# S5 maps: lag products and DRAM copies moved into the third MLP; norm squares first; results stored by token of the chunk

## Chip, cores and metric

One core of a Trainium2 chip runs the whole kernel as one program. The metric is the device time of one execution in microseconds. A profile of one execution goes with it; its times are us from the start of the profiled span.

## What is computed

A trunk of four layers over 256 tokens with 1024 channels. Each layer is a mixer and an MLP, each between two norms (`h += norm(mixer(norm(h)))`, the same for the MLP). The mixers are gated spatial mixing, pooling, latent attention and an S5 state-space layer; the change concerns what is prepared for the last one. Cut to that:

```
def rmsnorm(x, g):
    return x * rsqrt(mean(x * x, axis=-1) + 1e-6) * g

for i in range(4):
    z = mixer[i](rmsnorm(h, norm_g[i, 0]))
    h = h + rmsnorm(z, norm_g[i, 1])
    z = rmsnorm(h, norm_g[i, 2])
    z = square(relu(z @ w_up[i])) @ w_down[i]        # 1024 -> 4096 -> 1024
    h = h + rmsnorm(z, norm_g[i, 3])

def s5_mixer(h, ...):       # 64 groups of 16 channels, a complex state of 64 each
    dt = exp(log_dt); ab = exp(lam * dt); f = (ab - 1) / lam
    bu = (f * b) @ u                                  # per group
    x[t] = ab * x[t - 1] + bu[t]                      # scan over the tokens
    y = real(c @ x) + d_skip * u
    y = gelu(y)
    return (y @ w_glu_a) * sigmoid(y @ w_glu_b)
```

## The kernel before

The sublayers run one after another: `Gmlp`, `Mlp` 0, `Pooling`, `Mlp` 1, `Attention`, `Mlp` 2, `S5`, `Mlp` 3 (text below: first to fourth MLP). Tokens are in two blocks of 128. Every large product is made of three fp32r products (high and low parts), so each weight tile is loaded through SP's queue into one of three raw buffers and split by ACT (high part, L341) and DVE (low part, L342) into one of eight weight places. An MLP has eight groups of 512 hidden channels: `up_units` (L296 through `mm3`, into `mm`) and `down_units` (into `acc`), 22 us a group.

`boundary` (L1765) runs a sublayer's body, and then its last products for block 1, beside which block 0 is already normed, added and lifted (transposed) for the next sublayer; block 1 follows within the next body, after a first product of block 0 (`head`).

S5 doesn't scan token by token. It works in chunks of eight tokens and needs three sets of maps that depend on its parameters alone: `d_f` (into the state), `d_m` (within a chunk) and `d_e` (out of the state), 4 MB each in DRAM. `Tables` makes them as background work, a generator that `Core.tick` steps between the matmul units by an estimated clock: `yield 14` asks for a pause of 14 us by that clock. Its work is emitted in the middle of the MLPs' work; then a scheduler that runs a timing model fixes the order of each engine's instructions at build time. An emission under `high_priority(offset=-LATER)` counts as 500 instructions later than it stands.

`Tables.maps` (L1660) loops over 16 chunks of groups. For each, POOL loads `bo`, `bt`, `pb`, computes `e` and `cb` (complex products, `cmul`, L1553 to L1558) and `f`, and stores `f` to `d_f` and part of `e` to `d_out` (L1690). After every second chunk, `lags` (L1712) multiplies `e` with `cb` of two chunks on PE, eight small fp32 products a step (16 records in the trace, 128x128 with 32 weight columns), into the one buffer `pf`; ACT copies it to `lags`, and `place` (L1724) arranges it on POOL and stores it to `d_lag`. At the end eight copies within DRAM make `d_m` from `d_lag` (L1706) and four make `d_e` from `d_out` (L1709). `emit` drains the background before the third MLP, so all of it is emitted by then. `S5.stream` loads maps from `d_m` and `d_e` straight into the eight weight places, ahead of use.

S5 needs `h` with tokens in chunk order. `reorder` (L449), emitted in the third MLP, stores `h` to `d_h` on POOL's queue and loads it back through `in_chunks`, whose first dimension is the four tokens s, the second 32 chunks j. `finish` (L459) stores the result through the same view, per block two halves of 512 columns, one on SP's queue and one on ACT's.

The norm behind a sublayer is `add_normed` (L394): `t` = z * g on DVE (L404), `sumsq` of z on ACT (L355) inside `rstd`, a short chain for the root (L366 to L384), `h` += t * q (L408). z is in PSUM except for S5.

## Time and profile before

| | us |
|---|---|
| median of 3 runs | 1115.44 (1115.24 to 1116.12) |
| the profiled execution | 1114.36 |
| its span | 1112.6 |
| PE busy | 1013.0 (91%) |
| DVE busy | 749.7 (67%) |
| ACT busy | 546.6 (49%) |
| POOL busy | 391.5 (35%) |
| DMA | 233.97 MB, 210 GB/s on the mean |

PE is the engine of the matrix products; most of the time it is the one that the others feed. Its idle time is therefore read first, by who released it; then the stretches in which it ran with a lowered clock; then the stages in which no product runs.

### The profile page before, as it was taken

The numbers are of one execution on the slowest core, as the hardware profiler recorded it, in microseconds if no ns is written. First come the engines' busy times: TensorE is split into PE (matmuls) and PEld (weight loads), VectorE is DVE, ScalarE is ACT, GpSimd is POOL, SyncE is SP. The second block draws the span as 40 slices with busy tenths as digits, with TensorE's granted clock in tenths as the row PEclk, the third lists the DMA queues.
The fourth block names the chain that finished last, engine by engine and source line by source line (L and its number), as shares of the span: only waits on it lengthen the run. The fifth ranks groups of instructions, "written<-read, shape, count | busy, mean of one in ns | idle before, by whom it ended". The sixth has DMA issues, their size and how long they took to land.

```text
span 1112.6 us, 16304 instructions
## 1 busy us (share of the span) xinstructions
PE 1013.0 (91%) x6345; PEld 888.9 (80%) x6345; DVE 749.7 (67%) x1127; ACT 546.6 (49%) x818; POOL 391.5 (35%) x592
## 2 busy tenths in 40 slices
PE   7898999999689998988799799999985998999994
PEld 5886998997579887877687688999863777899983
DVE  5879999755986773657875665656569577454552
ACT  6946464443464443434454455545423466354531
POOL 4000002612879999899889430000003000000000
PEclk9999999999789998999999989999998999999998
DMA  9665475667576665665763798764576444646431
GB/s 333 233 232 189 152 256 197 204 243 268 182 252 234 217 219 183 231 211 174 247 207 120 242 391 232 246 220 157 218 307 248 151 153 157 220 157 221 156 112 38
DMA packets 82606, 233.97 MB, mean 210 GB/s; under 512 B 6320, under 2 KB 9648, under 8 KB 80736
## 3 DMA queue, kind: packets, MB, share of 16 engines
q1 hardware_dynamic: 67256, 182.73, 47.7%
q0 software_dynamic: 14720, 49.60, 13.4%
q8 instruction: 50, 0.82, 0.3%
q10 hardware_dynamic: 552, 0.59, 0.1%
q14 instruction: 28, 0.23, 0.1%
HBM read 218.48 MB, written 27.00 MB: 221 GB/s over the span
## 4 chain that ended last, share of the span: by engine, by line
PE 57%; POOL 15%; DVE 12%; DMA 7%; ACT 4%; issue 3%; SPq 0%; DVEq 0%; POOLq 0%; ACTq 0%
PE acc L296 29%; PE mm L296 26%; DVE w L342 3%; DMA raw<-in_a_w_in 2%; POOL tmp L1557 2%; DMA d_f<-f 2%; DVE s L1273 2%; DMA raw<-in_w_down 1%; ACT w L341 1%; DMA raw<-in_w_up 1%; POOL tmp L1554 1%; PE pf L296 1%; DVE h L408 1%; ACT junk L355 1%; DVE w L340 1%
## 5 line engine op out<-in xcount | busy, mean ns | idle before, releaser
L342 DVE TENSOR_TENSOR w<-raw,w 128x1024 fp32r<-128x1024 f32 (+3 forms) x304 | 379.0, 1277 | 163.9 <-ACT w L341 162.8
L341 ACT ACTIVATE w<-raw 128x1024 fp32r<-128x1024 f32 (+3 forms) x304 | 309.0, 1044 | 239.6 <-PE acc L296 131.9
L296 PE MATMUL acc<-w,h1hi 128*128 128x512 f32 (+1 forms) x1312 | 403.0, 391 | 3.7 <-ACT h1hi L341 3.1
L296 PE MATMUL mm<-zhi,w 128*128 128x256 f32 x1920 | 357.1, 286 | 3.4 <-DVE s L823 2.4
L296 PEld LDWEIGHTS mm<-zhi,w 128*128 128x128 f32 x1920 | 304.9, 194 | 6.8 <-DVE s L823 2.6
L296 PEld LDWEIGHTS acc<-w,h1hi 128*128 128x128 f32 x1312 | 244.8, 190 | 54.2 <-ACT h1hi L341 4.8
L296 PE MATMUL mm<-zlo,w 128*128 128x256 f32 x960 | 273.4, 285 | 0.0
L296 PE MATMUL acc<-w,h1lo 128*128 128x512 f32 (+1 forms) x656 | 253.6, 391 | 1.5 <-DVE h1lo L342 1.5
L296 PEld LDWEIGHTS mm<-zlo,w 128*128 128x128 f32 x960 | 185.9, 194 | 1.5 <-issue 0.4
L296 PEld LDWEIGHTS acc<-w,h1lo 128*128 128x128 f32 x656 | 124.4, 190 | 28.7 <-DVE h1lo L342 2.4
L631 DVE TENSOR_TENSOR s<-s 128x512 f32<-128x512 f32 x56 | 43.3, 773 | 61.1 <-ACT s L630 61.1
L630 ACT ACTIVATE s<-mm 128x512 f32<-128x512 f32 x56 | 33.4, 596 | 73.3 <-PE mm L296 71.1
L342 DVE TENSOR_TENSOR h1lo<-s,h1hi 128x512 fp32r<-128x512 f32 x60 | 54.1, 904 | 21.4 <-ACT h1hi L341 21.4
L341 ACT ACTIVATE h1hi<-s 128x512 fp32r<-128x512 f32 x60 | 45.3, 757 | 27.4 <-DVE s L631 25.5
L1275 POOL MEMSET t<- 128x32 f32 x2 | 0.3, 168 | 151.6 <-DVE h L408 151.6
L296 PE MATMUL mm<-w,zhi 128*128 128x512 f32 x128 | 42.1, 411 | 2.6 <-DVE zlo L342 2.1
L355 ACT ACTIVATE junk<-acc 128x512 bf16<-128x512 f32 x28 | 16.7, 595 | 56.0 <-DVE t L404 55.9
L404 DVE TENSOR_TENSOR t<-acc,bc 128x512 f32<-128x512 f32 x28 | 19.0, 686 | 36.1 <-PE acc L296 36.1
L296 PE MATMUL acc<-w,zhi 128*128 128x512 f32 (+2 forms) x128 | 38.4, 382 | 1.6 <-ACT w L339 1.6
L431 PE MATMUL mm<-ident,t 128*128 128x128 f32 x86 | 14.2, 303 | 24.3 <-DVE t L421 19.7
L328 POOL DMA_DIRECT2D bc<-in_norm_g x15 | 8.4, 558 | 78.8 <-DVE t L404 30.5
L431 PEld LDWEIGHTS mm<-ident,t 128*128 128x128 f32 x86 | 11.2, 157 | 27.5 <-issue 25.8
(304 smaller groups left out, 1227.4 us busy)
## 6 DMA issues: line engine op xcount, KB each, us to landing
raw<-in_w_up SPq DMA_DIRECT2D x64, 1024.0 KB, 5.2
raw<-in_w_down SPq DMA_DIRECT2D x64, 1024.0 KB, 5.1
bc<-in_norm_g POOLq DMA_DIRECT2D x15, 512.0 KB, 4.7
raw<-in_a_w_in SPq DMA_DIRECT2D x7, 1024.0 KB, 8.9
bt<-in_k_bt POOLq DMA_DIRECT2D x16, 256.0 KB, 4.5
raw<-in_a_w_out SPq DMA_DIRECT2D x4, 1024.0 KB, 6.2
d_out<-e POOLq DMA_DIRECT2D x16, 256.0 KB, 2.8
d_pb<-d_pw POOLq DMA_DIRECT2D x8, 512.0 KB, 8.8
```

The source lines that it names most:

```text
L296: return self.nc.tensor.matmul(out, lhsT, rhs, start=start, stop=stop)
L340: return i, nc.vector.scalar_tensor_tensor(lo, src, gain, hi.bitcast(F32), op0=ALU.mult, op1=ALU.subtract)
L341: i = nc.scalar.activation(hi, src, AF.Copy)
L342: return i, nc.vector.tensor_tensor(out=lo, in0=src, in1=hi.bitcast(F32), op=ALU.subtract)
L355: self.nc.scalar.activation(self.junk[:, 0:x.shape[-1]], x, AF.Square, scale=scale, bias=shift, accum_out=ss[:, i:i + 1])
L404: nc.vector.tensor_tensor(tn, zn, gn, op=ALU.mult)
L408: nc.vector.scalar_tensor_tensor(hn, tn, q, hn, op0=ALU.mult, op1=ALU.add)
L431: self.nc.tensor.transpose(ps[:, k * 128:(k + 1) * 128], z[:, k * 128:(k + 1) * 128], self.ident)
L630: nc.scalar.activation(s, state[f], AF.Relu)
L631: nc.vector.tensor_tensor(s, s, s, op=ALU.mult)
L1273: tt = lambda o, x, y, op: nc.vector.tensor_tensor(o, x, y, op=op)
L1557: eng.tensor_tensor(t, xr, yi, op=ALU.mult)
```

## The change

Six things. (1) `maps` no longer multiplies lags: `e` and `cb` lie in one tile `ec` (704 columns), which is stored whole to `d_ec`. (2) A new generator `within` waits for `late`, set when the third MLP begins; it then fetches two chunks of `ec` at a time (one step ahead), multiplies the lags, places them, and after every second step makes a quarter of `d_e` by two copies within DRAM; there is a pause of 6 us after each part. At its end the eight copies make `d_m`. (3) The background is drained not before the third MLP but after that MLP's sixth up-projection (g == 6). (4) `reorder` loads `h` back in four pieces of 32 partitions a block. (5) `finish` stores each half block in four such pieces. (6) `add_normed` emits the squares before the products with the gain.

```diff
--- before.py
+++ after.py
@@ -27,6 +27,7 @@
 LN_2 = Fraction("0.69314718055994530941723212145817656807550013436")
 MAGIC = 1.5 * 2.0 ** 23
 TURN_MAX = 0.5 - 2.0 ** -24
+EC = 704
 FMAX = float(np.finfo(np.float32).max)
 
 N_W = 8
@@ -38,6 +39,7 @@
 DEPTH = 2
 N_MAPS = 3
 MAPS_US = 14
+LAGS_US = 6
 LATER = 500
 WARM_S5 = 7.5
 
@@ -212,7 +214,7 @@
         self.background = None
         self.ends = {}
         self.recent = []
-        self.shallow = False
+        self.shallow = self.late = False
         self.weights = Weights(self)
         nc = self.nc
         self.eps = self.const.tile([128, 1], F32, name="eps")
@@ -355,10 +357,10 @@
             self.nc.scalar.activation(self.junk[:, 0:x.shape[-1]], x, AF.Square, scale=scale, bias=shift, accum_out=ss[:, i:i + 1])
         return [ss[:, i:i + 1] for i in range(len(parts))]
 
-    def rstd(self, parts, inner=None, outer=None):
+    def rstd(self, sums, inner=None, outer=None):
 
         nc = self.nc
-        a, b = self.sumsq(parts, D ** -0.5)
+        a, b = sums
         v = self.tiny("v")
         if inner is None:
             nc.vector.tensor_scalar(v, a, b, EPS, op0=ALU.add, op1=ALU.add)
@@ -399,17 +401,18 @@
             inner, outer = self.tiny("r4"), self.tiny("r2")
             nc.vector.tensor_tensor(outer, r, r, op=ALU.mult)
             nc.vector.tensor_tensor(inner, outer, outer, op=ALU.mult)
+        ss = self.sumsq(z, D ** -0.5)
         t = self.tp.tile([128, D], F32, name="t")
         for tn, zn, gn in zip(halves(t), z, halves(g)):
             nc.vector.tensor_tensor(tn, zn, gn, op=ALU.mult)
         with self.chain():
-            q = self.rstd(z, inner, outer)
+            q = self.rstd(ss, inner, outer)
             for hn, tn in zip(halves(self.h[b]), halves(t)):
                 nc.vector.scalar_tensor_tensor(hn, tn, q, hn, op0=ALU.mult, op1=ALU.add)
 
     def factor(self, b):
 
-        return self.rstd(halves(self.h[b]))
+        return self.rstd(self.sumsq(halves(self.h[b]), D ** -0.5))
 
     def scaled(self, b, g, r=None, out=None):
 
@@ -453,14 +456,18 @@
         for b in range(NB):
             nc.gpsimd.dma_start(out=d[b * 128:(b + 1) * 128], in_=self.h[b])
         for b in range(NB):
-            nc.gpsimd.dma_start(out=self.h[b], in_=in_chunks(d)[b])
+            for s in range(4):
+                nc.gpsimd.dma_start(out=self.h[b][sl32(s)], in_=in_chunks(d)[b][s])
         self.chunked = True
 
     def finish(self, out):
+
+        nc = self.nc
         for b in range(NB):
-            o = in_chunks(out)[b] if self.chunked else out[b * 128:(b + 1) * 128]
-            for n, queue in enumerate((self.nc.sync, self.nc.scalar)):
-                queue.dma_start(out=o[..., 512 * n:512 * n + 512], in_=self.h[b][:, 512 * n:512 * n + 512])
+            for n, queues in enumerate(((nc.sync,) * 4, (nc.scalar,) * 4)):
+                c = slice(512 * n, 512 * n + 512)
+                for s, queue in enumerate(queues):
+                    queue.dma_start(out=in_chunks(out)[b][s][:, c], in_=self.h[b][sl32(s), c])
 
     def z_parts(self):
         hi = self.xp.tile([128, 8, 256], F32R, name="zhi")
@@ -677,6 +684,8 @@
         for g in range(1, NG):
             k.run(self.up_units(g), side)
             side = [(5.0, self.factors)] if g == 1 else ()
+            if self.i == 2 and g == 6:
+                k.drain()
             if g == 1 and self.next is not None:
                 self.next.start()
             w = self.take()
@@ -1439,7 +1448,7 @@
         self.d_pw = k.dram.tile([2, 8, 16, 256], F32, name="d_pw")
         self.d_pb = k.dram.tile([128, 2, 16, 256], F32, name="d_pb")
         self.d_lag = k.dram.tile([8, 128, 512], F32, name="d_lag")
-        self.d_out = k.dram.tile([128, 32, 2, 128], F32, name="d_out")
+        self.d_ec = k.dram.tile([128, 16, EC], F32, name="d_ec")
 
     def small(self, name, *shape):
         return self.k.pre_p.tile([128, *shape], F32, name=name)
@@ -1663,9 +1672,6 @@
         k, nc, a = self.k, self.nc, self.a
         fr, fi = self.f
         pr, pi = self.powers
-        lg = self.small("lg", 512)
-        nc.gpsimd.memset(lg, 0.0)
-        before, made = None, None
         for ch in range(16):
             qs = slice(2 * ch, 2 * ch + 2)
             bo = self.small("bo", 192)
@@ -1677,8 +1683,9 @@
             tmp = self.small("tmp", 256)
             fb = lambda t: t[:, qs, None].to_broadcast([128, 2, 16])
             self.cmul((ov[:, 0], ov[:, 1]), (bv[:, 0], bv[:, 1]), (fb(fr), fb(fi)), tmp[:, 0:32].rearrange("p (q c) -> p q c", q=2))
-            e, cb = k.mp.tile([128, 2, 2, 9, 16], F32, name="e"), k.mp.tile([128, 2, 2, 2, 16], F32, name="cb")
-            nc.gpsimd.memset(cb, 0.0)
+            ec = k.mp.tile([128, EC], F32, name="ec")
+            e, cb = self.parts_of(ec)
+            nc.gpsimd.memset(ec[:, 576:EC], 0.0)
             for g in range(2):
                 hs = slice(64 * g, 64 * g + 64)
                 nc.gpsimd.tensor_copy(cb[hs, :, :, g], ov[hs])
@@ -1687,27 +1694,50 @@
             self.cmul([e[:, :, r, 1:9] for r in range(2)], (wide(2), wide(3)), (pw(pr), pw(pi)), tmp.rearrange("p (q i c) -> p q i c", q=2, c=16))
             nc.gpsimd.tensor_copy(e[:, :, :, 0], bv[:, 2:4].rearrange("p n q c -> p q n c"))
             nc.gpsimd.tensor_scalar(e[:, :, 1], e[:, :, 1], -1.0, None, op0=ALU.mult)
-            nc.gpsimd.dma_start(out=self.d_out[:, qs], in_=e[:, :, :, 1:9].rearrange("p q r i c -> p q r (i c)"))
-            if made is not None:
-                self.place(lg, *made)
-                made = None
+            nc.gpsimd.dma_start(out=self.d_ec[:, ch], in_=ec)
             f = self.small("f", 4, 2, 64)
             self.cmul([f[:, :, r] for r in range(2)], (pb[:, 0], pb[:, 1]), (bt[:, 0], bt[:, 1]), tmp.rearrange("p (s m) -> p s m", s=4))
             nc.gpsimd.dma_start(out=k.d_f[:, 4 * ch:4 * ch + 4], in_=f.rearrange("p s r m -> p s (r m)"))
             yield MAPS_US
-            if ch % 2:
-                with k.tc.high_priority(offset=-LATER):
-                    made = ch // 2, self.lags((before, (cb, e)))
-            before = cb, e
             yield 0
-        self.place(lg, *made)
+
+    def parts_of(self, ec):
+
+        return ec[:, 0:576].rearrange("p (q r i c) -> p q r i c", q=2, r=2, c=16), ec[:, 576:EC].rearrange("p (r q g c) -> p r q g c", r=2, q=2, g=2)
+
+    def within(self):
+
+        k, nc = self.k, self.nc
+        lg = self.small("lg", 512)
+        nc.gpsimd.memset(lg, 0.0)
+        fetched = {}
+
+        def fetch(n):
+            fetched[n] = []
+            for ch in (2 * n, 2 * n + 1):
+                ec = k.mp.tile([128, EC], F32, name="ec")
+                nc.gpsimd.dma_start(out=ec, in_=self.d_ec[:, ch])
+                fetched[n].append(self.parts_of(ec)[::-1])
+
+        fetch(0)
+        yield LAGS_US
+        for n in range(8):
+            with k.tc.high_priority(offset=-LATER):
+                t = self.lags(fetched[n])
+            if n < 7:
+                fetch(n + 1)
+            yield LAGS_US
+            self.place(lg, n, t)
+            if n % 2:
+                r, g = n // 4, n // 2 % 2
+                src = self.d_ec[64 * g:64 * g + 64, :, 0:576].rearrange("p h (q r x) -> p h q r x", q=2, r=2)
+                for q in range(2):
+                    nc.gpsimd.dma_start(out=k.d_e[64 * r:64 * r + 64, 2 * q + g:64:4], in_=src[:, :, q, r, 16:144])
+            yield LAGS_US
         for i, s in enumerate(TOKEN):
             w = self.d_lag.rearrange("n (g c) f -> c (n g) f", c=16)[:, :, 256 * (s // 4) + 32 * (3 - s % 4):][:, :, 0:128]
             nc.gpsimd.dma_start(out=k.d_m[16 * i:16 * i + 16], in_=w)
-        for r in range(2):
-            for g in range(2):
-                nc.gpsimd.dma_start(out=k.d_e[64 * r:64 * r + 64, g:64:2], in_=self.d_out[64 * g:64 * g + 64, :, r])
-        yield 0
+            yield 3
 
     def lags(self, pairs):
 
@@ -1740,6 +1770,9 @@
         yield from self.recurrence()
         self.k.early = False
         yield from self.maps()
+        while not self.k.late:
+            yield 0
+        yield from self.within()
 
 
 def constants():
@@ -1797,7 +1830,7 @@
             while k.early:
                 k.step()
         if isinstance(s, Mlp) and s.i == 2:
-            k.drain()
+            k.late = True
         boundary(k, s, n)
     k.finish(out)
 
```

## Rows read from the trace of the kernel before

**Rows 1.** Page, part 2: busy tenths of the span in 40 slices of 27.8 us.
```profile
PE   7898999999689998988799799999985998999994
POOL 4000002612879999899889430000003000000000
```

**Rows 2.** Waits of PE: engine, line, releaser: us in total, times, longest.
```profile
PE pf L296 <- POOL e L1555: 15.4, 7, 5.4
...
PE pf L296 <- POOL e L1689: 3.2, 1, 3.2
```

**Rows 3.** Timeline of PE, 380 to 525 us: start, duration, instruction [idle before].
```profile
382.75 0.43 PE L296 MATMUL pf<-e,cb 128*32 128x128 f32 x8 [0.77 <-POOL e L1555]
...
429.31 0.66 PE L296 MATMUL pf<-e,cb 128*32 128x128 f32 x8 [5.43 <-POOL e L1555]
...
478.02 0.66 PE L296 MATMUL pf<-e,cb 128*32 128x128 f32 x8 [2.99 <-POOL e L1555]
...
502.33 0.41 PE L296 MATMUL pf<-e,cb 128*32 128x128 f32 x4 [0.52 <-POOL e L1555]
...
521.13 0.43 PE L296 MATMUL pf<-e,cb 128*32 128x128 f32 x8 [2.96 <-POOL e L1555]
```

**Rows 4.** Stretches, second and fourth MLP: busy us (instructions) by engine, clock, DMA, GB/s.
```profile
320.00:518.20 198.20, 188.45 (x1168) 165.80 (x1168) 124.54 (x124) 87.54 (x115) 185.14 (x277) 0.96 0.63 211
922.07:1098.60 176.53, 175.69 (x1096) 158.79 (x1096) 93.89 (x113) 79.06 (x100) 0.00 (x0) 1.00 0.46 157
```

**Rows 5.** The second MLP's stretch, tile pf alone: PE, weight loads, ACT.
```profile
320.00:518.20 198.20, 5.86 (x64) 2.00 (x64) 1.09 (x4) 0.96 0.63 211
```

**Rows 6.** Stretches behind two waits: columns as in rows 4.
```profile
430.00:435.00 5.00, 5.00 (x30) 4.99 (x30) 0.00 (x0) 0.00 (x0) 4.21 (x7) 0.68 0.43 157
520.00:525.00 5.00, 3.87 (x21) 3.68 (x22) 4.66 (x11) 1.45 (x5) 4.81 (x7) 0.70 0.81 265
```

**Rows 7.** Timelines of ACT and PE at the start of the third and fourth MLP.
```profile
637.16 1.06 ACT L341 ACTIVATE w<-raw 128x1024 fp32r<-128x1024 f32 x1 [6.89 <-DMA raw<-in_w_up]
...
642.26 1.94 PE L431 MATMUL mm<-ident,t 128*128 128x128 f32 x8 [8.22 <-DVE t L421]
...
922.07 1.23 PE L431 MATMUL mm<-ident,t 128*128 128x128 f32 x8 [2.10 <-DVE t L421]
```

**Rows 8.** Stretches at the start of the third MLP: columns as in rows 4.
```profile
640.00:645.00 5.00, 2.74 (x13) 2.66 (x14) 4.64 (x8) 1.60 (x3) 2.52 (x4) 0.50 1.03 420
645.00:650.00 5.00, 5.00 (x17) 3.95 (x17) 2.44 (x3) 2.22 (x3) 3.91 (x6) 0.67 1.02 406
```

**Rows 9.** DMA issues, whole run, then 600 to 700 us: KB each, us to landing.
```profile
raw<-in_w_up SPq DMA_DIRECT2D x64, 1024.0 KB, 5.2
...
d_e<-d_out POOLq DMA_DIRECT2D x4, 1024.0 KB, 10.4
d_m<-d_lag POOLq DMA_DIRECT2D x8, 512.0 KB, 14.2
```

**Rows 10.** The end: one stretch (as in rows 4); ACT's stores, ns min/median/max.
```profile
1107.00:1108.00 1.00, 0.00 (x0) 0.00 (x0) 0.00 (x0) 0.00 (x0) 0.00 (x0) 0.50 0.27 104
...
L463 ACTq DMA_DIRECT2D out<-h x2: 552/850/1147, 1093.1 to 1103.3; - x2
```

**Rows 11.** Page, part 5: the norm's squares; busy, mean ns, idle before, releaser.
```profile
L355 ACT ACTIVATE junk<-acc 128x512 bf16<-128x512 f32 x28 | 16.7, 595 | 56.0 <-DVE t L404 55.9
```

**Rows 12.** Low priority, and S5's first products: DVE timeline, tile pf, PE timeline.
```profile
200.91 0.83 DVE L1644 TENSOR_TENSOR t<-t 128x256 f32<-128x256 f32 x2
...
L1651 PE MATMUL pf<-ident,t x4: 270/270/272, 238.8 to 239.9; 128*128 128x128 f32 x4
...
829.30 1.12 PE L296 MATMUL mm<-raw,zlo 128*32 128x128 f32 x32 [1.35 <-issue]
...
835.04 1.47 PE L1343 MATMUL acc<-w,zlo 128*32 128x128 f32 x42
...
861.14 1.72 PE L296 MATMUL pf<-w,t 128*32 128x128 f32 x25 [8.71 <-DVE t L1273]
```

## What the change should do, by the rows

> **What bounds the kernel now.** I began with the busy slices of the page [rows 1]. TensorE (PE) is full in most slices, so what can be gained lies in its idle time and in stretches where it runs slowly; GpSimd (POOL) is nearly full from slice 11 to slice 21 and does nothing in most of the third MLP. Next the waits of PE, grouped by releaser [rows 2]: PE stood 15.4 + 3.2 = 18.6 us before the small "pf" matmuls until POOL had written `e`. These are the `lags` products, which the schedule placed into PE's order before POOL was done. The timeline of PE [rows 3] gives the places: 0.77, 5.43, 2.99 and 0.52 us in the second MLP, 2.96 us at its end, where attention begins; the other 5.9 us lie in pooling and attention. Then two MLPs with the same matrix work, from the transposes of their second block to the last product [rows 4]: 198.20 us for the second MLP, 176.53 us for the fourth. The 21.7 us between them is what the S5 preparation costs there. Two more places stand out: the 8.22 us before the third MLP's transposes [rows 7], and the end, where results are stored at 104 GB/s with the DMA engines 27% busy [rows 10].
>
> **Second MLP: -18 us.** The change takes the products out. (a) The four waits go: 0.77 + 5.43 + 2.99 + 0.52 = 9.7 us. (b) The products go: 64 records with 5.86 us of busy time in this stretch [rows 5]; they run one after another, so I take 5.5. (c) After the two long idles PE was granted 0.68 of full speed in 430 to 435 us [rows 6], a mean of its levels of 1.2 and 2.4 GHz, where the fourth MLP had 1.00 throughout [rows 4]: 0.32 x 5 = 1.6 us, and about as much after the 2.99 us wait, scaled by its length to 1.0; 2.7 us together. Sum 17.9. The bound above is the whole 21.7 us. Below, DVE's splitting of weights could come next: it is busy for 124.54 of 198.20 us [rows 4], and would be 69% busy in 180 us. PE recorded no long wait for a split here, so DVE keeps up on the mean; I bound the loss at half, 9 us. What else changes in the maps (one whole store of `ec` for the store of its part, no `place`, no wait for `lags`) only shortens POOL's list, whose end nobody on the path waits for.
>
> **Attention and pooling: -6 us.** At the start of attention 2.96 us goes, and with it the slow clock behind it (0.70 in 520 to 525 us [rows 6], 0.30 x 3.9 busy us = 1.2). What remains of the 18.6 us is 5.9, of which most stands in front of work that waits for DVE anyway; I count 2. The bounds are 2 (DVE's chain through the latents is late next) and 12 (all of the waits, their clock and the products' own time).
>
> **The boundary to the third MLP: -9.5 us.** PE waits 8.22 us for `t` of the second block. On ACT the square root of that chain sits behind a weight split, and the split waited 6.89 us for its weights [rows 7]. The DMA engines are full (share 1.03, in 640 to 645 us still [rows 8]): the four copies of `d_e` inside DRAM, 1 MB each and 10.4 us to land, have just been issued, and the w_up load shares with them; over the whole run such a load lands in 5.2 us [rows 9]. The change takes these copies away from here, spreads them by halves over the third MLP, and leaves only the two chunks of the first fetch. What is late next is the chain itself, acc to squares to root to `h` to transposes: the same boundary of the fourth MLP waits 2.10 us [rows 7]. So 8.2 - 2.1 = 6.1 us, plus the clock: 0.67 in 645 to 650 us, and 0.50, the lower level, over the 2.74 busy us before [rows 8], 0.33 x 5 + 0.50 x 2.74 = 3.0; after the 2.10 us wait it was not lowered. Sum 9.1, and 0.4 for DMA relief behind it. Bounds: 3 (the load is late for its slot, not for traffic) and 11.
>
> **Third MLP: +9 us.** All 128 records move here, where PE is full, so they cost in full: 2 x 5.86 = 11.7 us above, or, since with both chunks at hand the sixteen of one step run in a row (8 in 0.43 us [rows 3]), 16 x 0.43 = 6.9 below. I take 8. The new wait is for fetched data: sixteen loads of 352 KB on POOL's queue. I price a landing at the 5.2 us of a 1 MB weight load [rows 9]. The first steps are fetched one step (three pauses of 6 us) ahead, so nothing waits; the steps that the drain emits in a lump have no such lead, and the second buffer of each fetch is freed only by the products before (three buffers). I put 1 us there, 0 to 15.6 (three steps at 5.2). Behind a waiting DMA on POOL stand the bias and gain broadcasts and `place`; POOL is idle here [rows 1], and PE needs none of them in the MLP. The traffic is another 6 MB read, in a stage where the engines had room after the burst of its first 20 us. The reload of `h` in chunk order, now eight DMAs, is needed some 20 us later and hidden by the MLP's products; uncovered it would cost its landing, 5 us and up.
>
> **S5: +2 us.** Before, the maps were complete long ahead; S5's first product ran at 829.30 us and the first one with a map at 835.04 [rows 12]. Now the last three steps and the eight `d_m` copies are emitted with the sixth up-projection, two of eight groups before the MLP's end (2 x 176.5 / 8 = 44 us), and the products at low priority. What such a priority costs is shown once: the transposes of `spread` were ready at 201.7 (end of DVE's L1644) and ran at 238.8 [rows 12], 37 us later. So the last steps run as the MLP ends; then `place`, one store, eight copies, whose landing I take as 5 us rather than the 14.2 of the crowded stretch [rows 9]: `d_m` is there about 16 us after S5's first product instead of long before. PE's next hard wait, until 861.14 for DVE's scan [rows 12], ends 32 us behind that product and hides nearly all of it. I take 2, bounds -1 and 12.
>
> **The end: -3.3 us.** 27% of sixteen engines is four: each store has an outermost dimension of four (the token of the chunk). Cut into pieces of 32 partitions, the 512 KB can go over all: 6 us of transfer at 104 GB/s become 1.5 us at four times the rate. Against that stand three more issues on each queue, 0.55 us at the least [rows 10], 1.7 us, partly beside the transfer. Net 3.3; bounds 0 and 5. The Trainium skill agrees on the four ("DMA: Bandwidth & Descriptors", "Why a DMA increments its semaphore by 16 and not by 1": the slowest dimension sets how many engines a DMA gets). But its section "Rules for kernel authors" there speaks against cutting: transfers of disjoint partitions serialize, one of 128 partitions is better. By the first rule the end is shorter by my 3.3 us, by the second it stays as it is; the share of 27% bears out the first.
>
> **Squares before products in the norm: -0.5 us.** ACT's squares waited for DVE's `t` on the same bank, 55.9 us over the kernel [rows 11], nearly all off the path. Now `t` waits for the squares; on the path it is the same two operations in the other order, the root's first step a little earlier at best. Bounds -2 and +2.
>
> **Sum.** -18 - 6 - 9.5 + 9 + 2 - 3.3 - 0.5 = -26.3. The profiled execution took 1114.4 us, its span 1112.6 and 1.8 around it; 1114.4 - 26.3 = 1088. The median of the runs is 1.1 higher, so 1089.
>
> **Rivals.**
> (A) PE's wait moves with the products: instead of POOL it waits for the fetched chunks. For it: PE takes its instructions in order, and three steps come in a lump. Against: the first five are fetched early. Price 15.6 us instead of the 1 counted, and 3 of slow clock: 1107. Chance 0.13.
> (B) The maps come too late for S5; this ends slower. The chain from the last product to the last load of a map is serial: fetch, product, `place`, store, eight copies, eight loads of 1 MB. At the landings of the crowded stretch (14.2 for a `d_m` copy [rows 9], as much again for the store, 10 for each of two fetches) the last map lies about 80 us behind the MLP's end. It decides from about 40 us on, where DVE's scan no longer covers it; every us beyond is PE's, the weights behind it on SP's queue and the eight weight places held by maps too. To lose all of 26 us it must come 66 us late; at 80 us, 1089 + 40 - 2 = 1127. Against: the DMA engines are half empty then. Chance 0.08.
> (C) The second MLP is bound by splits, DVE being slowed by POOL's work that stays: half of the 18 us, 1098. Chance 0.13.
> (D) The boundary keeps its stall, the load being late for its slot: 1089 + 6 = 1095. Chance 0.08.
> (E) The end does not shorten, since pieces serialize: 1089 + 3.3 = 1092; small beside the rest. Chance 0.10. The second rule of the skill named above would do this.
>
> **How the numbers follow.** My forecast, 1089 give or take 10, has 0.48. A, C, D, E lie between 1092 and 1107 and are faster than before too. The range is 1076 (the good bounds of MLP, attention and end together) to 1107 (A included); B and sums better than 1076 are left out. A difference of 0.2%, 2.2 us, is about what a measurement of this kernel can tell from none. Faster 0.88, same 0.03 (B half way, or A with C), slower 0.09 (B and a bad order of instructions).
>
> **What would show it.** In the profile after: no PE wait for POOL's `e`; the second MLP near 180 us by the stretch of rows 4; the wait before the third MLP's transposes near 2 us and granted clock 1.00 behind it; "pf" products of `ec` in the third MLP with about 8 us, and no idle before them; the third MLP longer by these; S5's first use of a map at most 10 us later against its first product; the store at the end with a DMA share well above 0.27. It is wrong if PE waits for `ec`, for maps in S5, or if the second MLP stays above 189 us.

## The result, and the profile after

The changed kernel takes 1131.07 us (median of 4, 1126.15 to 1133.07) beside 1115.34 for the kernel before: a ratio of 1.0154, 95% interval 1.0118 to 1.0189. It is 16 us slower where I had forecast 26 us faster. The profiled execution took 1130.65 us, its span is 1128.7.

The stages, from the timelines of PE (us; a stage runs to the start of the next one; the columns e2 to e9 are experiments, told below):

| stage, from | before | after | e2 | e3 | e6 | e9 |
|---|---|---|---|---|---|---|
| start of the span | 320.0 | 319.7 | 320.3 | 318.2 | 320.5 | 319.1 |
| second MLP: transposes of its second block | 201.5 | 181.4 | 181.1 | 180.6 | 181.0 | 181.0 |
| attention: first 384-column product | 120.8 | 132.0 | 130.9 | 126.5 | 115.2 | 115.5 |
| third MLP: transposes of its second block | 187.0 | 206.9 | 190.8 | 186.3 | 205.8 | 191.3 |
| S5: its first product | 92.8 | 102.5 | 93.4 | 91.0 | 90.4 | 88.7 |
| fourth MLP: transposes, to the end | 190.5 | 186.2 | 185.9 | 186.2 | 186.0 | 185.3 |

After minus before: -0.3 - 20.1 + 11.2 + 19.9 + 9.7 - 4.3 = 16.1, the difference of the spans. The second MLP and the end gave what was expected, 24.4 us; attention, the third MLP and S5 took 40.8.

The stretches of the changed kernel's profile (columns as in [rows 4]): the second MLP, which answers to the first line there; the start of attention; 100 us of the third MLP; S5 where it waits for maps; the fourth MLP; the last stores.

```profile
319.68:501.04 181.36, 178.93 (x1104) 162.00 (x1104) 128.31 (x119) 85.98 (x110) 170.74 (x230) 0.98 0.66 222
...
523.00:550.00 27.00, 12.48 (x32) 8.61 (x33) 16.10 (x30) 4.73 (x9) 24.32 (x45) 0.57 0.66 220
...
700.00:800.00 100.00, 100.00 (x615) 84.71 (x614) 50.56 (x47) 45.42 (x51) 16.39 (x30) 1.00 0.58 198
...
842.00:900.00 58.00, 33.97 (x434) 25.80 (x434) 34.73 (x73) 18.82 (x24) 11.74 (x8) 0.79 0.90 347
...
942.48:1119.00 176.52, 176.39 (x1094) 159.65 (x1095) 93.76 (x113) 79.12 (x100) 0.00 (x0) 0.99 0.47 158
...
1125.50:1126.50 1.00, 0.00 (x0) 0.00 (x0) 0.00 (x0) 0.00 (x0) 0.00 (x0) 0.50 0.84 256
```

In the second MLP PE idles for 2.4 us instead of 9.8. In attention it is busy for 12.48 of 27 us, at a granted clock of 0.57. The third MLP's line is the deceptive one: PE is 100% busy at full clock, and yet the stage is longer.

The waits of PE (columns as in [rows 2]). POOL's `e` is gone from the list; other names have come.

```profile
PE acc L1352 <- DMA w<-d_m: 11.1, 2, 10.6
PE mm L434 <- DVE t L1053: 9.5, 2, 7.2
...
PE mm L298 <- DVE t L1068: 5.0, 1, 5.0
PE pf L298 <- DMA ec<-d_ec: 4.6, 2, 2.7
```

**Attention.** Timelines of the changed kernel: DVE at the copy into `krt` (the rotary keys' tile), and POOL at the same moment.

```profile
538.05 0.59 DVE L1068 COPY t<-mm 64x128 f32<-64x128 f32 x2 [9.87 <-POOL t L1037]
...
536.83 0.72 POOL L1564 TENSOR_TENSOR ec<-ec,tmp 128x256 f32<-128x256 f32 x1
537.49 0.52 POOL L1037 MEMSET t<- 128x512 f32 x1
```

And the same two instructions in the kernel before:

```profile
532.42 0.52 POOL L1028 MEMSET t<- 128x512 f32 x1
...
545.48 0.58 DVE L1059 COPY t<-mm 64x128 f32<-64x128 f32 x2
```

POOL zeroes `krt` somewhere in its list of map work. Before, the zeros were there 12.5 us ahead of their use. After, DVE is ready for the copy at 538.05 - 9.87 = 528.2, 17 us earlier, because the second MLP is shorter; POOL comes to the zeros 5 us later than before. So the gain upstream, and POOL's own delay, turned a slack of 12.5 us into a wait of 9.87.

**Third MLP.** The timeline of PE in one step of `lags`, then a step that ran in a row.

```profile
742.04 0.41 PE L298 MATMUL pf<-ec 128*32 128x128 f32 x2
742.38 0.39 PE L298 MATMUL mm<-zlo,w 128*128 128x256 f32 x1
742.69 0.41 PE L298 MATMUL pf<-ec 128*32 128x128 f32 x2
743.03 0.38 PE L298 MATMUL mm<-zhi,w 128*128 128x256 f32 x1
743.34 0.41 PE L298 MATMUL pf<-ec 128*32 128x128 f32 x2
...
825.30 0.65 PE L298 MATMUL pf<-ec 128*32 128x128 f32 x16
```

A small product (two records) and a main product together take 742.69 - 742.04 = 0.65 us, and 743.34 - 742.69 the next time. Ahead of the step a main product starts every 0.12 us (740.63, 740.75, 740.87), so each small one between them costs 0.53 us; all sixteen records of a step take 0.65 us in a row. Thirty products stand so, one by one, in the MLP (the rest of the third step and the three steps behind it; between the 512-column products of the down-projection a pair takes 0.76 us instead of 0.23, again 0.53 more): 30 x 0.53 = 15.9 us. No idle time is recorded, so the loss hides in "busy".

**The end of the third MLP and S5.** PE's timeline: the last step, the warm-up products (`zeros`), the first use of a `d_m` map, the product behind DVE's scan; then POOL's issues of the copies to `d_e` and `d_m`.

```profile
826.42 0.41 PE L298 MATMUL pf<-ec 128*32 128x128 f32 x4 [0.48 <-ACT lags L1751]
829.57 0.63 PE L298 MATMUL pf<-ec 128*32 128x128 f32 x12 [2.74 <-DMA ec<-d_ec]
830.66 0.59 PE L298 MATMUL pf<-zeros 128*128 128x512 bf16 x1 [0.46 <-ACT lags L1751]
831.47 8.57 PE L298 MATMUL pf<-zeros 128*128 128x512 bf16 x33 [0.22 <-issue]
...
867.51 1.94 PE L1352 MATMUL acc<-w,zlo 128*32 128x128 f32 x32 [10.58 <-DMA w<-d_m]
...
881.98 0.31 PE L298 MATMUL pf<-w,t 128*32 128x128 f32 x3
...
605.54 6.04 POOL L1735 DMA_DIRECT2D d_e<-d_ec  x8
...
838.32 6.06 POOL L1739 DMA_DIRECT2D d_m<-d_lag  x8 [2.03 <-DMA d_lag<-lg]
```

The last step runs after the MLP's last product, the warm-up needs its one `pf` buffer and stands behind it, the `d_m` copies are issued 8 us later still, and the first map is used 27.5 us behind S5's first product instead of 5.7 [rows 12].

**The boundary** to the third MLP answers to [rows 7]: the wait of 8.22 us is gone.

```profile
633.02 1.25 PE L434 MATMUL mm<-ident,t 128*128 128x128 f32 x8 [0.20 <-DVE t L424]
```

### The profile page after: what moved, and what is told of

The parts are those of the page before. It is cut to its first block, busy times and chain, and to the rows that moved or that the text cites. A ratio compares the mean times of both kernels' runs of the same rounds, so it can differ in the third digit from the quotient of the medians.

```text
span 1128.7 us, 16359 instructions
## 1 busy us (share of the span) xinstructions
PE 1028.6 (91%) x6344; PEld 895.4 (79%) x6345; DVE 748.9 (66%) x1127; ACT 547.9 (49%) x818; POOL 400.6 (35%) x618
## 4 chain that ended last, share of the span: by engine, by line
PE 55%; POOL 21%; DMA 8%; DVE 7%; issue 5%; ACT 3%; SPq 0%; DVEq 0%; POOLq 0%; ACTq 0%
PE acc L298 28%; PE mm L298 25%; POOL tmp L1566 3%; POOL tmp L1563 2%; DVE w L344 2%; DMA d_f<-f 2%; DMA d_m<-d_lag 2%; POOL ec L1696 1%; DMA w<-d_m 1%; POOL ec L1565 1%; DMA d_ec<-ec 1%; DVE h L411 1%; POOL f L1565 1%; POOL ec L1562 1%; ACT junk L357 1%
## 5 line engine op out<-in xcount | busy, mean ns | idle before, releaser
L343 ACT ACTIVATE w<-raw 128x1024 fp32r<-128x1024 f32 (+3 forms) x304 | 309.5, 1043 | 226.4 <-PE acc L298 131.6
L344 DVE TENSOR_TENSOR h1lo<-s,h1hi 128x512 fp32r<-128x512 f32 x60 | 53.7, 897 | 20.1 <-ACT h1hi L343 20.1
L1719 POOL DMA_DIRECT2D ec<-d_ec x16 | 9.0, 563 | 152.4 <-PE pf L298 152.4
L344 DVE TENSOR_TENSOR h1lo<-mm,h1hi 128x512 fp32r<-128x512 f32 (+2 forms) x26 | 15.8, 613 | 26.8 <-ACT h1hi L343 26.7
L298 PEld LDWEIGHTS mm<-w,zhi 128*128 128x128 f32 x128 | 25.4, 204 | 9.7 <-DVE zlo L344 2.8
```

Source lines behind the costliest of these rows:

```text
L298: return self.nc.tensor.matmul(out, lhsT, rhs, start=start, stop=stop)
L343: i = nc.scalar.activation(hi, src, AF.Copy)
L344: return i, nc.vector.tensor_tensor(out=lo, in0=src, in1=hi.bitcast(F32), op=ALU.subtract)
```

## The experiments

My theory after this profile: (1) the zeroing of `krt` costs attention 11 us; (2) the low priority of the `lags` products makes them run mixed with main products, and late; the warm-up and S5's maps are late for the same cause. Rivals: the products' own time, the added DMA traffic, the fetches, the order of the squares. Times are medians. The kernel before was timed again beside each group of runs, with medians of 1115.5 (e1 to e4), 1110.0 (e5 to e8), 1111.3 (e9 to e12) and 1113.8 us (e13, e14); so ratios to it are compared across groups.

### e1: krt zeroed by DVE

```
-        nc.gpsimd.memset(krt, 0.0)
+        nc.vector.memset(krt, 0.0)
```

> The changed kernel with one edit: the zeroing of krt is done by DVE instead of POOL. Theory (attention lost 11 us because DVE waited 9.87 us at 538 us for POOL's zeroing, which stood behind the maps in POOL's list): that wait is gone, the stretch from the latents to the third MLP's transposes falls from 132.0 to about 121, and the kernel from 1131 to about 1120. Rival (DVE or PE is short of something else there, such as slow clock or POOL's port traffic): the stretch stays above 128 us and the time within 3 us of 1131.

Measured: 1126.22 us, ratio 1.0096 (1.0062 to 1.0131); the stretch from attention to the third MLP 131.6 us. The wait is gone and the stretch is as long as before: neither theory nor rival in its wording. PE's timeline has a new wait:

```profile
573.57 0.64 PE L298 MATMUL pf<-ec 128*32 128x128 f32 x4 [16.48 <-DMA ec<-d_ec]
```

The first `lags` products stand in PE's order within attention, and the chunk that they need is fetched by POOL, behind its list of maps. One late item of POOL's list had covered another.

### e2: lags at the priority of the program order

```
-            with k.tc.high_priority(offset=-LATER):
-                t = self.lags(fetched[n])
+            t = self.lags(fetched[n])
```

> The changed kernel with one edit: the lags products are given their place in the program order instead of low priority, so that the eight of a step stand in a row on PE. Theory (the low priority both delays the steps and mixes each step's products one by one with main products, 4.3 us a step instead of 0.65): the third MLP from its transposes to the last main product falls from 192.3 to about 183 us, the warm-up behind it starts at once, and the first use of a map comes at most 10 us after S5's first product instead of 27.5; in all 1131 - 9 - 5.6 - 9.7, about 1107. Rival 1 (PE now waits in its order for the fetched chunks): waits of pf for ec of 3 to 5 us a step, the MLP stays at 190 or more. Rival 2 (the MLP is bound by the splitting of weights or by DMA): 190 or more with PE idle for w.

Measured: 1102.87 us, ratio 0.9882 (0.9842 to 0.9922). Five of the steps now run in a row in the third MLP:

```profile
710.13 0.39 PE L298 MATMUL acc<-w,h1lo 128*128 128x512 f32 x1
710.45 0.65 PE L298 MATMUL pf<-ec 128*32 128x128 f32 x16
711.02 0.39 PE L298 MATMUL mm<-zhi,w 128*128 128x256 f32 x1
711.25 0.28 PE L298 MATMUL mm<-zlo,w 128*128 128x256 f32 x1
...
700.00:800.00 100.00, 100.00 (x674) 89.48 (x673) 56.40 (x53) 50.16 (x56) 22.95 (x48) 1.00 0.73 268
```

PE is 100% busy in these 100 us here too, but finishes 674 records instead of 615. From its transposes to the end of its last main product the MLP takes 814.05 - 632.23 = 181.8 us (after: 825.3 - 633.0 = 192.3); the warm-up follows at once; the first map is used 5.75 us behind S5's first product, as before; S5 takes 93.4 us. That one line of the change was worth 30 us by the ratios. Rivals 1 and 2 fall: PE waits 5.2 us for `ec`, once, in attention.

### e3: no lags products

```
-                    k.mm(ps[sl32(2 * n + q), 0:128], cb..., e..., r == 0, r == 1)
...
-        nc.scalar.activation(t..., ps[:, 0:128], AF.Copy)
+        for n, (cb, e) in enumerate(pairs):
+            nc.scalar.activation(t..., e[:, 0, 0, 0:8]..., AF.Copy)
```

> The changed kernel without the lags products: ACT copies a part of each fetched chunk instead of PE's result (these products are left out of the computation); all fetches, place, stores and copies stay. It prices what the products alone do. Theory: the third MLP takes 177 to 180 us instead of 192.3, as the fourth does, S5's maps are there in time, and the kernel takes about 1131 - 14 - 5.6 - 9.7 = 1102, attention's loss of 11 us staying. Rival (the new DMA traffic of 12 MB or POOL's work slows the third MLP): 188 us or more in the third MLP though the products are gone.

Measured: 1092.93 us, ratio 0.980 (0.976 to 0.984), 9 us below what was expected (5.5 of them in attention, which I had left at 132.0). The third MLP takes 802.57 - 625.24 = 177.3 us with all the fetches, copies and POOL's work still there: traffic is not what slowed it. Against e2 the products cost 181.8 - 177.3 = 4.5 us (five whole steps and most of a sixth, in rows); against the changed kernel 192.3 - 177.3 = 15.0 mixed, near the 15.9 counted above.

### e4: another tile for the warm-up

```
-        ps = self.pf.tile([128, 512], F32, name="pf")
+        ps = self.bank()
```

> The changed kernel with one edit: the 34 warm-up products ahead of S5 write a tile of the mm buffers instead of the one pf buffer, which the last lags hold until 830.66 us. Theory (the 5.6 us there and the 9.7 us in S5 are one cause, the last lags: the maps that need them come no earlier): S5's first product moves ahead by about 5 us, but the first use of a map stays about 60 us before the same point, the wait for d_m grows from 10.6 to about 16 us, and the time stays within 2 us of 1131. Rival (two separate costs that add): the time falls by 5 to 6 us to about 1125.

Measured: 1135.64 us, ratio 1.0175 (1.0138 to 1.0212), no different from the changed kernel. S5's first product came 2 us earlier (837.98; 3.4 earlier if counted from the MLP's transposes), less than the 5 expected, and the wait for maps grew as the theory said:

```profile
870.98 1.93 PE L1352 MATMUL acc<-w,zlo 128*32 128x128 f32 x32 [15.60 <-DMA w<-d_m]
```

So the warm-up's 5.6 us and S5's 9.7 us are one chain, not two costs.

### e5 and e6: products tied into the third MLP, and krt by DVE

```
-            with k.tc.high_priority(offset=-LATER):
+            with k.after([k.recent[-1]]):
                 t = self.lags(fetched[n])
```

> The changed kernel with one edit: each step's eight lags products are tied behind the main product that the code emitted last, in place of low priority. All 64 products then stand in the third MLP, eight in a row, none in attention. Theory (attention in e2 lost 5.24 us to a fetched chunk that POOL's full list delivers late, besides the 10 us for krt): the wait for ec in attention is gone, the third MLP grows by the three blocks moved into it, 3 x 0.65 = 2 us, to about 184, and the kernel falls from e2's 1102.9 to about 1100. Rival (steps that start later make d_m late again): a wait for w from d_m in S5, 1105 or more.

Measured (e5): 1100.57 us, ratio 0.9904 (0.9877 to 0.9931), as e2 within the intervals. No wait for `ec` is left in attention (128.2 us). The third MLP, up to its last main product, takes 811.86 - 629.53 = 182.3 us with all eight steps in it: against e3 the 64 products cost 5.0 us in rows (8 x 0.77 = 6.2 us of PE's time; PE idles 1.2 us more in e3). No wait for `d_m` in S5, so its rival falls.

> As e5, and krt is zeroed by DVE. Theory (krt's late zeroing is the rest of attention's loss, and in e1 its gain was eaten by a 16.48 us wait for a chunk that POOL's list delivered late): with no lags product left in attention that wait can't come back, the stretch from the latents to the third MLP's transposes falls to 121 or less, and the kernel to about 1100 - 8 = 1092. Rival (attention has another bound, POOL slowing DVE): the stretch stays above 126, 1098 or more.

Measured (e6): 1097.41 us, ratio 0.9867 (0.9815 to 0.9919). Attention and boundary fall from 128.2 to 115.2 us, 13 less: the late zeros were attention's loss. But the stage of the third MLP takes 205.8 us, 14.5 more than e5's 191.3, by a wait that was in no profile so far. (The four runs lie between 1088.94 and 1100.79 us, and the profile is of the longest: the wait need not be as long in each.) POOL's issues, ACT and PE in e6:

```profile
610.05 6.05 POOL L1735 DMA_DIRECT2D d_e<-d_ec  x8
...
623.14 0.53 POOL L457 DMA_DIRECT2D d_h<-h  x1 [1.10 <-DVE w L344]
...
639.98 3.41 POOL L460 DMA_DIRECT2D h<-d_h  x7 [14.44 <-DMA d_h<-h]
...
646.65 0.63 ACT L357 ACTIVATE junk<-h 128x512 bf16<-128x512 f32 x1 [19.65 <-DMA h<-d_h]
...
649.14 1.22 PE L298 MATMUL acc<-w,h1hi 128*128 128x512 f32 x2 [11.71 <-ACT h1hi L343]
```

`h` goes to DRAM and back for the new token order. Its store lands 16 us after its issue, behind the eight `d_e` copies (4 MB) issued shortly before; ACT stands in its order before the squares of the reloaded `h`; the split that PE needs is behind them.

### e7: the order of the eight products

```
-        for r in range(2):
-            for n, (cb, e) in enumerate(pairs):
-                for q in range(2):
+        for n, (cb, e) in enumerate(pairs):
+            for q in range(2):
+                for r in range(2):
```

> e2's kernel with the order of the eight products of a step changed: the two that add up in the same 32 columns stand one behind the other, where e2 goes through the four column groups first. Theory (a 32-column product alone takes 0.33 us; the eight take 0.65 us in a row only because products of different column groups run side by side, and mixed with main products they can't): a block takes 1.3 to 2.6 us instead of 0.65, the third MLP 3 to 10 us more than e2's 181.8, the time 1106 to 1113. Rival (what costs in the mix is the change between a small and a full product, not the loss of neighbours): the block stays at 0.65 us and the time at 1103.

Measured: 1098.83 us, ratio 0.9893 (0.9866 to 0.992), as e2. A step still takes as long:

```profile
706.64 0.66 PE L298 MATMUL pf<-ec 128*32 128x128 f32 x16
707.24 0.39 PE L298 MATMUL mm<-zhi,w 128*128 128x256 f32 x1
```

My theory, by which this order makes a step take 1.3 to 2.6 us, falls; the rival stands: the change between small and main products costs.

### e8: the end alone, in the kernel before

```
-            for n, queue in enumerate((self.nc.sync, self.nc.scalar)):
-                queue.dma_start(out=o[..., 512 * n:512 * n + 512], in_=self.h[b][:, 512 * n:512 * n + 512])
+            for n, queue in enumerate((self.nc.sync, self.nc.scalar)):
+                c = slice(512 * n, 512 * n + 512)
+                for s in range(4):
+                    queue.dma_start(out=in_chunks(out)[b][s][:, c], in_=self.h[b][sl32(s), c])
```

> The kernel before with the end alone changed: each block of results stored in pieces of 32 partitions by the token of the chunk, everything else as before. Theory (the 4.3 us that the changed kernel gained behind the fourth MLP's transposes are the stores'): 1115.4 - 4.3, about 1111, with the stretch from those transposes to the end at 186 instead of 190.5. Rival (they come from the squares placed before the products, or the stores of pieces serialize): 190 and 1115.

Measured: 1105.40 us, ratio 0.9963 (0.9938 to 0.9987): -4.1 us. From the fourth MLP's transposes to the end 185.5 us instead of 190.5. Four pieces of 64 KB, issued within 1.72 us, end the run 5.0 us after the first of them; the one store of 256 KB per queue took 10.0 (1102.6 to 1112.6).

```profile
1099.46 1.72 SPq L464 DMA_DIRECT2D out<-h  x4
1100.13 1.75 ACTq L464 DMA_DIRECT2D out<-h  x4
```

### e9: the d_e copies behind the stores of lags

To e6:

```
-            self.place(lg, n, t)
+            p = self.place(lg, n, t)
...
+                with k.after([p.ins]):
                     for q in range(2):
                         nc.gpsimd.dma_start(out=k.d_e[...], in_=src[:, :, q, r, 16:144])
...
-        nc.gpsimd.dma_start(out=self.d_lag[n], in_=lg)
+        return nc.gpsimd.dma_start(out=self.d_lag[n], in_=lg)
```

> As e6, and each pair of d_e copies is queued on POOL behind the store of the lags of its step, so that the eight copies no longer stand ahead of the reordering of h. Theory (attention's 12 us did come in e6, and were given back as a wait of 11.71 us in the third MLP: ACT stood 19.65 us before the squares of h, which came back from DRAM late because the d_e copies filled the DMA engines): ACT's wait for h falls below 8 us, the 11.71 us wait of PE goes, and the kernel comes 8 to 11 us below e6, at a ratio near 0.978 to before. Rival (h is late for its own round trip, whatever is in front): the wait stays near 11 us and the ratio at 0.987.

Measured: 1083.90 us, ratio 0.9755 (0.9717 to 0.9792), faster than both kernels. The 11.71 us are gone, and the stores of `h` land 5.1 us (median) after their issue. ACT's wait for `h`:

```profile
627.13 0.63 ACT L357 ACTIVATE junk<-h 128x512 bf16<-128x512 f32 x1 [1.27 <-DMA h<-d_h]
```

### e10 and e11: what makes the mix dear

e10 takes `lags` on the upper halves of the numbers as bf16, e11 as full tiles of 128 columns in fp32 (the true sums are left out of it); both on the changed kernel, mixed as there.

```
-  k.mm(ps[sl32(2 * n + q), 0:128], cb..., e..., r == 0, r == 1)
+  k.mm(ps[sl32(2 * n + q), 0:128], cb....bitcast(BF16)[:, 1::2], e....bitcast(BF16)[:, 1::2], r == 0, r == 1)    (e10)
+  k.mm(ps[:, 0:128], e[:, q, r, 1:9]..., e[:, q, r, 0:8]..., True, True)                                      (e11)
```

> The changed kernel with the lags products taken on the upper halves of the numbers as bf16, 32 columns as before (so these products are rounded). The schedule still mixes them one by one with main products. If the type makes the change dear (fp32 among fp32r), a pair of one small and one main product in the up-projection takes well under the 0.65 us of the changed kernel, near 0.2. If the small tile makes it dear, it stays between 0.5 and 0.65 us.

> The changed kernel with each lags product as a full tile of 128 columns, fp32, started and ended by itself (its sums are thus left out of the computation). Mixed one by one as in the changed kernel. If the small tile makes the change dear, a small and a main product together take about 0.12 + 0.08 to 0.3 us; if the type does, 0.65 us as before.

PE's timelines, e10 and then e11:

```profile
740.95 0.23 PE L298 MATMUL pf<-ec 128*32 128x128 bf16 x1
741.11 0.38 PE L298 MATMUL mm<-zhi,w 128*128 128x256 f32 x1
741.42 0.23 PE L298 MATMUL pf<-ec 128*32 128x128 bf16 x1
```

```profile
740.23 0.38 PE L298 MATMUL pf<-ec 128*128 128x128 f32 x2
740.37 0.36 PE L298 MATMUL mm<-zhi,w 128*128 128x256 f32 x1
740.57 0.38 PE L298 MATMUL pf<-ec 128*128 128x128 f32 x2
```

A pair takes 0.47 us with bf16 in 32 columns (741.42 - 740.95), a little under the 0.5 that I had put as the lower bound for the tile, and 0.34 with fp32 in 128 columns, against 0.65 with fp32 in 32: the pair with a product four times as wide takes half the time. Less the 0.12 of the main product, the wide product costs 0.22 us in the mix, and eight of them in a row take 1.95, 0.24 each: mixing them costs nothing that shows. So it is the size of the tile that makes the mix dear, and the type less so (one run each: 1124.21 and 1115.83 us).

What is dear is the interruption, not the product. In e2 a step of eight small products stands behind the main product at 710.13. From there to the second main product behind the step, at 711.25, pass 1.12 us; without the step it would be 0.23 + 0.12. So the eight cost 0.77 us together, where a single one costs 0.53. The change there and back is therefore about 0.5 us, an estimate that holds if a small product costs no more alone than in a row. The Trainium skill ("TensorEngine Tiling (Array Packing)", section "Key Properties") states that a change of the tiling mode, and not just of the tile, drains TensorE. The trace agrees: the cost is there with 128x32 tiles among 128x128 ones, and not with 128x128 ones alone; the drain itself is in no record.

### e12, e13, e14: the squares first

e12 makes this part alone in the kernel before; e13 undoes it in the changed kernel, e14 in e9.

```
         t = self.tp.tile([128, D], F32, name="t")
+        ss = self.sumsq(z, D ** -0.5)
...
-            q = self.rstd(z, inner, outer)
+            q = self.rstd(ss, inner, outer)
```

> The kernel before with the squares of a norm placed ahead of its products with the gain, nothing else. My prediction: -0.5 us (between -2 and +2), so a ratio of 0.998 to 1.002. Rival (the order moves the instructions of ACT and DVE at every boundary and costs there): 1.005 or more.

> The changed kernel with the norm's products with the gain ahead of the squares again, as in the kernel before; nothing else. If the order of the squares costs by itself (e12: 0.35% of the kernel, some 4 us), the changed kernel falls by about 4 us, to a ratio near 1.012. If what e12 showed belongs to the schedule of the kernel before alone (its boundary to the third MLP, where ACT and DVE were late), it stays at 1.015.

> e9's kernel with the products ahead of the squares again. If the order of the squares costs by itself, the ratio falls from e9's 0.9755 to about 0.972; if not, it stays within 0.973 to 0.978.

Measured: e12 1116.91 us, 1.0035 (1.0008 to 1.0063); e13 1129.38 us, 1.0166 (1.0111 to 1.0221) beside the changed kernel's 1.0154; e14 1086.86 us, 0.9779 (0.974 to 0.9817) beside e9's 0.9755. In the changed kernel and in the mended one the order makes no difference that was measured. What it cost in the kernel before (attention and boundary take 125.1 us in e12's profile, before 120.8) belongs to that schedule: PE waits 7.5 us instead of 4.5 for `t` in attention, and 9.72 instead of 8.22 at the boundary. Why was not followed.

## Why the prediction was wrong

**Second MLP, -18: right.** -20.1, at clock 0.98; PE waits for POOL no more, and DVE's splits did not come next (rival C falls).

**Attention, -6: wrong, and the sentence that failed is "POOL's list, whose end nobody on the path waits for".** It stands under the second MLP in the prediction, and I applied it to attention too. I read that PE's wait for POOL's `e` would go, and not what else stands in POOL's order: the zeros of `krt`, the fetches of `ec`, the store and reload of `h`. Each has someone on the path behind it. With the zeros done by DVE (e6) attention and boundary together get 5.6 us shorter than before; forecast were 15.5 for the two.

**The boundary, -9.5: the wait went; my reason fits in part and was not tested.** The wait fell from 8.22 to 0.20 us, with the clock at 1.00. But the change did not spread the `d_e` copies over the third MLP: they need only the stored chunks, so all eight were issued together at 605.54, ahead of the boundary. What changed is where the w_up load stands that the split ahead of the root needs. Before, it was issued at 623.14, among the four copies (619.16 to 625.07), and landed after 13.9 us; in the changed kernel it was issued 9 us behind the last of them and landed after 7.5. The split then waits 1.26 us instead of 6.89. In e6 the copies stand 7 us before the transposes, behind the load, and PE waits 0.32 us there. This fits copies and load sharing the DMA engines, which was my reason; no run moved the copies alone in the kernel before, so it is not shown. What the copies did delay is the reload of `h`, which I had called hidden by the products, with 5 us and up if uncovered; uncovered in e6 it cost 11.7.

**Third MLP, +9: the products do cost PE's time, but the term was mis-sized, by their order.** I took 8 us because "the sixteen of one step run in a row", between 6.9 and 11.7. In rows they cost less, 5.0 (e5 against e3). Mixed they cost 15.0, above my upper bound. I had taken that bound from the second MLP before, where 60 of the 64 records ran in rows of two or four products [rows 3, 5]. The price of the mix stood in the same trace, in one place that I did not read. PE's timeline of the kernel before:

```profile
457.83 0.41 PE L296 MATMUL pf<-e,cb 128*32 128x128 f32 x2
458.17 0.39 PE L296 MATMUL mm<-zlo,w 128*128 128x256 f32 x1
458.48 0.41 PE L296 MATMUL pf<-e,cb 128*32 128x128 f32 x2
458.82 0.39 PE L296 MATMUL mm<-zhi,w 128*128 128x256 f32 x1
```

A single product and a main one take 458.48 - 457.83 = 0.65 us there too. What I did not ask is where low priority would put the products on a PE that is full.

**S5, +2: the step that failed is that DVE's scan hides the maps.** Both of its sizes were wrong. The maps came later: I had put `d_m` about 16 us behind S5's first product, and its first use came 27.5 behind it, 22 later than before, since low priority held the steps back, as e2 shows (the first whole one of the MLP starts at 762 us, the next ones about every 20, the last behind the MLP's last product). And the cover was shorter than the 32 us that I counted: ahead of the scan's product PE had idled 8.71 us [rows 12], and the products of the maps themselves, which stand before it in PE's order, now began those 22 us later. The scan's product runs at 881.98, 42 us behind S5's first product instead of 32, and no longer waits for the scan. S5 paid 9.7 us; 5.6 more were paid ahead of it by the warm-up, whose buffer I had not followed. The mechanism is rival B's, at a smaller size: 15.3 us in all instead of the 38 that B's 1127 us has in it. That 1127 lies near the measured 1131 is luck; the mix and attention make up the rest. Rival A's wait for chunks is there with 4.6 us, and 19.2 in e1 once the zeros no longer cover it.

**The end, -3.3: right.** -4.3, and -5.0 in e8's profile, the bound; rival E falls. The DMA engines are 84% busy at 256 GB/s in the last stores, where it was 27% and 104 [rows 10]; the pieces shorten the kernel by 4.1 us (1.4 to 6.9) in e8. Of the two rules of the Trainium skill that the prediction weighs ("DMA: Bandwidth & Descriptors", sections "Why a DMA increments its semaphore by 16 and not by 1" and "Rules for kernel authors"), the one on the slowest dimension decided here. One reading in the sum was off: 512 KB at 104 GB/s are 5.0 us, not 6. **Squares, -0.5:** none measured in the changed kernel.

With the order of the products, the zeros of `krt` and the place of the `d_e` copies mended (e9), the change brings 2.45%, 27 us. That is about the 26.3 forecast, but by other terms, so the nearness is luck. By the profiles: second MLP -20.5, attention and boundary -5.3, third MLP +4.3, S5 -4.1, end -5.2, start -0.9.

## What to carry to other kernels

Where work is moved to an engine that is full, price the order that it will get there and not only its duration: a small tile between full ones cost 0.53 us where eight in a row cost 0.77 together, and the profile called all of it busy. Look in the trace at hand for one place where that order already stands. Before writing that nobody waits for an engine's list, go through every instruction in it, with the slack that it has now; a gain upstream uses that slack up first. When a wait is taken away and the time stays, look for the next item of the same queue.

## What the runs showed of the hardware

At full clock one 128x32 fp32 product between two 128x128 products cost PE 0.53 us, eight in a row only 0.77 us together (e2), all of it recorded as busy time. Between fp32 and fp32r of the same tile size the mix cost nothing that shows (0.34 us a pair in e11, 0.12 of it the main product; eight of its full tiles in a row took 1.95). And a store of `h` (512 KB) landed 16 us after its issue behind 4 MB of copies within DRAM from the same queue (e6), where it took 5.1 without them (e9).
